# Two groups of small loads in a DMA-filled elementwise kernel on Trainium2

## The chip, the cores and the metric

The kernel runs on one core of a Trainium2 chip. The metric is the device time of one execution in microseconds (us). The kernel before took 1867.16 us in the median of 3 runs (1866.8 to 1867.26). The engines that matter here are VectorE (DVE), ScalarE (ACT), SyncE (SP), which does nothing but issue DMAs, and the sixteen DMA engines that carry out what SP issues.

## The reference

`pred` and `target` are 8192 x 8192 arrays of float32. The output is the Huber loss of each element:

```python
diff = pred - target
abs_diff = np.abs(diff)
return np.where(abs_diff <= 1.0, 0.5 * diff**2, abs_diff - 0.5)
```

Two arrays of 268 MB are read and one is written, with a few operations an element.

## The kernel before, in words

All three arrays are taken as flat and cut into 37 tiles of 128 rows. The list `widths` holds the columns of each: 9408 for tile 0, 12000 for tile 1, 14592 (`W`) for the next 34, and 6752 for the last. Tile `i` is one contiguous stretch of memory, so that a row is a contiguous run of 4 x width bytes.

One buffer, `mem`, takes 128 rows of 53184 columns of the on-chip memory. The functions `at_a(i)` and `at_b(i)` say where the pred and the target of tile `i` lie in it. Targets of even tiles start at column 0, those of odd tiles at 14592; preds of even tiles start at 29184, those of odd tiles end at 53184. The preds of two neighbouring tiles overlap in some columns (`covered`). The result of a tile is made in the place of its target, and is stored from there.

`load(i)` issues the DMAs of a tile on SP (line 80): pred, then target, each in one transfer of 7296 KB for a full tile, and in two parts for tiles 0, 34, 35 and 36. For the last tile both parts of pred go ahead of both parts of target. `store(i)` (line 85) writes the result, in one transfer, or two for the last tile.

`work(i, then)` computes a tile in pieces of some 5000 columns, of which each goes through five instructions: DVE subtracts (line 95), ACT takes the absolute value (96), DVE clamps it to 1 (100), ACT squares half of it (103), DVE combines the two with the maximum of (|d| - 0.5) and the square (107). `work` interleaves the pieces, and calls `then` behind the first subtractions, where the loads of the next tile are issued.

The order of the work is written out by hand (`manual_schedule`), and each engine runs its instructions in the order in which the program issues them. SP's order is therefore: the loads of tiles 0 and 1; then for each tile the store of the tile before, and the loads of the tile behind. An instruction of SP that waits holds up all that stand behind it. What each waits for is worked out by the framework from the columns that are read and written, and from the semaphores that it gives to the DMAs: eight of them, taken in turn. The loop is

```python
load(0)
load(1)
for i in range(n):
    if i > 0:
        store(i - 1)
    work(i, lambda: load(i + 1) if 0 < i < n - 1 else None)
store(n - 1)
```

Of the kernel before, what the change touches and what calls it, by code (L numbers as in the profile page):

```python
# [1 line left out]

# [4 lines left out]


@with_exitstack
def kernel(  # L10
    ctx: ExitStack,
    tc: tile.TileContext,
    pred: bass.AP,
    target: bass.AP,
    out: bass.AP,
):
    nc = tc.nc
    P = 128
    fp32 = mybir.dt.float32
    Alu = mybir.AluOpType  # L20
    Act = mybir.ActivationFunctionType
    SQRT_HALF = 0.70710678118654752

    total = pred.shape[0] * pred.shape[1] // P
    W = 14592
    GAP = 9408
    R = W - GAP
    widths = [GAP, W - R // 2] + [W] * 34
    widths.append(total - sum(widths))
    n = len(widths)  # L30
    starts = [sum(widths[:i]) * P for i in range(n)]

    def block(x, i):
        flat = x.rearrange("r m -> (r m)")
        return flat[starts[i] : starts[i] + P * widths[i]].rearrange("(p m) -> p m", p=P)

    pool = ctx.enter_context(tc.tile_pool(name="memory", bufs=1))
    mem = pool.tile([P, 3 * W + GAP], fp32, name="mem")

    def at_a(i):
        return 3 * W + GAP - widths[i] if i % 2 else 2 * W

    def at_b(i):
        return W if i % 2 else 0

    def covered(i):  # L50

        if i + 1 >= n:
            return (0, 0)
        lo = max(at_a(i), at_a(i + 1))
        hi = min(at_a(i) + widths[i], at_a(i + 1) + widths[i + 1])
        return (lo - at_a(i), hi - at_a(i)) if hi > lo else (0, 0)


    def parts(i):
        w = widths[i]  # L60
        if i == n - 3:
            return [(w - 2 * R, w), (0, w - 2 * R)]
        if i in (0, n - 2, n - 1):
            return halves(w)
        return [(0, w)]

    def halves(w):
        h = w // 32 * 16
        return [(0, h), (h, w)]

    def view(base, lo, hi):
        return mem[:, base + lo : base + hi]

    def load(i):
        order = [(x, part) for part in parts(i) for x in "pt"]
        if i == n - 1:
            order = [(x, part) for x in "pt" for part in parts(i)]
        for x, (lo, hi) in order:
            src, base = (pred, at_a(i)) if x == "p" else (target, at_b(i))
            nc.sync.dma_start(out=view(base, lo, hi), in_=block(src, i)[:, lo:hi])  # L80

    def store(i):
        w = widths[i]
        for lo, hi in halves(w) if i == n - 1 else [(0, w)]:
            nc.sync.dma_start(out=block(out, i)[:, lo:hi], in_=view(at_b(i), lo, hi))

    def split(lo, hi, size):
        k = -((lo - hi) // size)
        edges = [lo + (hi - lo) * j // k // 16 * 16 for j in range(k)] + [hi]
        return list(zip(edges[:-1], edges[1:]))  # L90


    def subtract(i, lo, hi, at):
        a, d = view(at_a(i), lo, hi), view(at_b(i), lo, hi)
        nc.vector.tensor_tensor(out=d, in0=a, in1=d, op=Alu.subtract)  # L95
        nc.scalar.activation(out=d, in_=d, func=Act.Abs)  # L96

    def square(i, lo, hi, at):
        d, t = view(at_b(i), lo, hi), view(at_a(i) + at, 0, hi - lo)
        nc.vector.tensor_scalar(  # L100
            out=t, in0=d, scalar1=-1.0, scalar2=1.0, op0=Alu.max, op1=Alu.min
        )
        nc.scalar.activation(out=t, in_=t, func=Act.Square, scale=SQRT_HALF)  # L103

    def combine(i, lo, hi, at):
        d, t = view(at_b(i), lo, hi), view(at_a(i) + at, 0, hi - lo)
        nc.vector.scalar_tensor_tensor(  # L107
            out=d, in0=d, scalar=-0.5, in1=t, op0=Alu.add, op1=Alu.max
        )

    def pieces(i, lo, hi):


        c0, c1 = covered(i)
        c0, c1 = max(lo, c0), min(hi, c1)
        if c1 <= c0:
            k = -((lo - hi) // (R // 2 if i < n - 1 else R // 4))
            return [], [(i, x, y, x) for x, y in split(lo, hi, -((lo - hi) // k))]
        x, y = (lo, c0) if c0 > lo else (c1, hi)
        m = max(c1 - c0, (y - x) // 32 * 16)  # L120
        rest = [(x, x + m), (x + m, y)] if y > x + m else [(x, y)]
        return [(i, c0, c1, x)], [(i, x, y, x) for x, y in rest]

    def work(i, then):

        todo, held = [], []
        for part in parts(i):
            first, rest = pieces(i, *part)
            todo += first + rest
            held += first  # L130
        mid, end = [], []
        if held:
            subtract(*todo.pop(0))
        then()
        while todo or mid or end or held:
            if todo:
                piece = todo.pop(0)
                subtract(*piece)
                mid.append(piece)
                if len(mid) < 2 and todo:  # L140
                    continue
            if mid:
                piece = mid.pop(0)
                square(*piece)
                end.append(piece)
                if len(end) < 2 and (todo or mid):
                    continue
            combine(*end.pop(0))
            mid += held
            held = []  # L150

    ctx.enter_context(tc.manual_schedule())

    load(0)
    load(1)
    for i in range(n):
        if i > 0:
            store(i - 1)
        work(i, lambda: load(i + 1) if 0 < i < n - 1 else None)
    store(n - 1)  # L160


# [1 line left out]
_INS = ['pred', 'target']  # L164
_OUTS = [((8192, 8192), 'float32')]


# [23 lines left out]
```

## Time and profile before

| | |
|---|---|
| median of 3 runs | 1867.16 us |
| the profiled execution | 1866.7 us |
| its span | 1864.9 us |
| DVE busy | 1408.3 us (76%) |
| ACT busy | 912.5 us (49%) |
| DMA moved | 805.37 MB, 432 GB/s over the span |
| DMA issues | 120, by their counts in the list of issues |

The page has the span in 40 slices, with a digit for the busy share of each engine in tenths and the rate of the DMA in GB/s. The chain of work that ended last goes back from the end to what released each step; in order of time, each row gives its start, its length and its engine. SPq is SP's queue: a row of it is the issue of a DMA, and the landing comes later. The list of issues gives the time from issue to landing. A view of several stretches gives, for each stretch, its length, the busy time of DVE, ACT and POOL, the clock of TensorE (not used here), the DMA's share and its rate.

### The profile page before, as it was taken

The page shows a single profiled execution, that of the slowest core. Times are in us where ns is not written, and L with a number is a line of the kernel's source. Part 1 is how long each engine was busy: PE and PEld are TensorE (multiplying, and loading weights), DVE is VectorE, ACT ScalarE, POOL GpSimd, SP SyncE. Part 2 cuts the span into 40 slices and gives each one's busy share as a digit, 9 for nine tenths or more (in the row PEclk, how much of TensorE's full clock was granted, in tenths as well). Part 3 has the DMA queues.
Part 4 walks back from the last instruction along what each step waited for, and adds up shares of the span by engine and source line. Part 5 has one row for each costly group of instructions (what it writes and reads, how often), then busy time and mean ns, then how long its engine had stood idle before and what let it go on. Part 6 is the DMA issues. An engine that isn't in the chain of part 4 may idle for free.

```text
span 1864.9 us, 960 instructions
## 1 busy us (share of the span) xinstructions
DVE 1408.3 (76%) x357; ACT 912.5 (49%) x239; POOL 0.2 (0%) x4
## 2 busy tenths in 40 slices
DVE  5677777777788777777778877777777887777986
ACT  3455444444555545444455554544445555454554
POOL 0000000000000000000000000000000000000000
DMA  9999999999999999999999999999999999999999
GB/s 421 418 436 431 436 431 432 437 427 436 438 428 434 439 428 435 438 429 433 438 428 436 438 428 435 438 428 436 438 427 437 436 429 437 435 429 436 428 437 393
DMA packets 17287, 805.37 MB, mean 432 GB/s; under 512 B 1920, under 2 KB 1920, under 8 KB 1920
## 3 DMA queue, kind: packets, MB, share of 16 engines
q1 hardware_dynamic: 17280, 805.31, 99.9%
q14 instruction: 7, 0.06, 0.0%
HBM read 536.87 MB, written 268.44 MB: 432 GB/s over the span
## 4 chain that ended last, share of the span: by engine, by line
DMA 56%; DVE 26%; ACT 13%; issue 4%; another core or an unknown queue 1%; SPq 0%; DVEq 0%
DMA mem<-in_target_dram 32%; DMA out_dram<-mem 24%; DVE mem L107 11%; DVE mem L95 11%; ACT mem L103 8%; ACT mem L96 4%; DVE mem L100 3%; SPq L80 0%; DVEq L95 0%
## 5 line engine op out<-in xcount | busy, mean ns | idle before, releaser
L96 ACT ACTIVATE mem<-mem 128x5184 f32<-128x5184 f32 (+8 forms) x119 | 459.2, 3874 | 756.3 <-DVE mem L95 756.2
L95 DVE TENSOR_TENSOR mem<-mem 128x5184 f32<-128x5184 f32 (+8 forms) x119 | 558.5, 4743 | 336.2 <-DMA mem<-in_target_dram 336.2
L107 DVE SCALAR_TENSOR_TENSOR mem<-mem 128x5184 f32<-128x5184 f32 (+8 forms) x119 | 564.4, 4745 | 74.5 <-ACT mem L103 70.6
L103 ACT ACTIVATE mem<-mem 128x5184 f32<-128x5184 f32 (+8 forms) x119 | 456.7, 3864 | 169.2 <-DVE mem L100 169.2
L100 DVE TENSOR_SCALAR mem<-mem 128x5184 f32<-128x5184 f32 (+8 forms) x119 | 292.0, 2453 | 34.9 <-ACT mem L96 29.9
L96 ACT ACT_TABLE_LOAD x1 | 1.3, 1283 | 14.6 <-DMA mem<-in_target_dram 14.6
L175 POOL MEMSET const-bfloat16-1.0<- 128x1 bf16 x1 | 0.1, 103 | 0.0
L175 POOL MEMSET const-uint8-127<- 128x1 uint8 x1 | 0.1, 102 | 0.0
L175 POOL MEMSET const-float32-0.0<- 128x1 f32 x1 | 0.1, 100 | 0.2 <-issue 0.2
L175 POOL MEMSET const-float32-1.0<- 128x1 f32 x1 | 0.1, 99 | 0.0
## 6 DMA issues: line engine op xcount, KB each, us to landing
out_dram<-mem SPq DMA_DIRECT2D x34, 7296.0 KB, 26.5
mem<-in_pred_dram SPq DMA_DIRECT2D x32, 7296.0 KB, 28.7
mem<-in_target_dram SPq DMA_DIRECT2D x32, 7296.0 KB, 34.4
mem<-in_pred_dram SPq DMA_DIRECT2D x2, 3648.0 KB, 27.6
mem<-in_target_dram SPq DMA_DIRECT2D x2, 3648.0 KB, 25.5
mem<-in_pred_dram SPq DMA_DIRECT2D x1, 6000.0 KB, 36.8
mem<-in_target_dram SPq DMA_DIRECT2D x1, 6000.0 KB, 51.5
out_dram<-mem SPq DMA_DIRECT2D x1, 6000.0 KB, 24.6
```

The source lines that it names most:

```text
L95: nc.vector.tensor_tensor(out=d, in0=a, in1=d, op=Alu.subtract)
L96: nc.scalar.activation(out=d, in_=d, func=Act.Abs)
L100: nc.vector.tensor_scalar(out=t, in0=d, scalar1=-1.0, scalar2=1.0, op0=Alu.max, op1=Alu.min)
L103: nc.scalar.activation(out=t, in_=t, func=Act.Square, scale=SQRT_HALF)
L107: nc.vector.scalar_tensor_tensor(out=d, in0=d, scalar=-0.5, in1=t, op0=Alu.add, op1=Alu.max)
L175: nc = _bacc.Bacc("TRN2", target_bir_lowering=False, num_devices=1)
```

## The change

A function `few_rows(at)` is added. It issues eight loads on SP, of 1, 2, 4, 6, 8, 10, 12 and 14 rows and of 16, 32 and so on to 128 columns, from the first rows of `pred` into `mem` from column `at` on, side by side. They are read by nothing. It is called twice: behind the loads of tile 1, ahead of the first store, into the columns behind tile 0's target (`GAP` is 9408); and behind the loads of the last tile, ahead of the store of tile 35, into the columns behind the last tile's pred.

```diff
+    def few_rows(at):
+        for k, rows in enumerate((1, 2, 4, 6, 8, 10, 12, 14)):
+            w = 16 * (k + 1)
+            nc.sync.dma_start(
+                out=mem[0:rows, at : at + w], in_=block(pred, 0)[0:rows, 0:w]
+            )
+            at += w
...
     load(0)
     load(1)
+    few_rows(GAP)
     for i in range(n):
         if i > 0:
             store(i - 1)
-        work(i, lambda: load(i + 1) if 0 < i < n - 1 else None)
+        if i == n - 2:
+            load_last = lambda: (load(i + 1), few_rows(2 * W + widths[n - 1]))
+            work(i, load_last)
+        else:
+            work(i, lambda: load(i + 1) if 0 < i < n - 1 else None)
     store(n - 1)
```

The instructions of DVE and ACT and their order are the same in both kernels; SP has 16 DMAs more.

## The prediction

> **What bounds the kernel now.** I read the page's slices first, then the DMA queues, the chain, the queue of SP (the engine that issues every DMA), and last the stretches in which the rate of the DMA sinks.
>
> ```profile
> DVE  5677777777788777777778877777777887777986
> ACT  3455444444555545444455554544445555454554
> ...
> DMA  9999999999999999999999999999999999999999
> GB/s 421 418 436 431 436 431 432 437 427 436 438 428 434 439 428 435 438 429 433 438 428 436 438 428 435 438 428 436 438 427 437 436 429 437 435 429 436 428 437 393
> ...
> q1 hardware_dynamic: 17280, 805.31, 99.9%
> ```
>
> VectorE and ScalarE have room in every slice; the DMA has none in any, and its queue is 99.9% busy. So the end moves by what is taken from or given to the DMA, and time in which its sixteen engines have nothing is lost for good. The steady rate comes from the chain: the store issued at 607.61 lands at 634.09, the one at 710.94 at 737.42, and two tiles (six transfers of 7296 KB) take 103.33 us between: 17.22 us each, 434 GB/s. The mean is 432.
>
> Next, the two places of the change. The first answer below is SP's queue around the first store, the second around the end, the third the chain at the start, the fourth the rates.
>
> ```profile
> 44.92 0.35 SPq L85 DMA_DIRECT2D out_dram<-mem  x1
> 58.21 0.33 SPq L80 DMA_DIRECT2D mem<-in_pred_dram  x1
> 66.40 0.33 SPq L80 DMA_DIRECT2D mem<-in_target_dram  x1
> ```
>
> ```profile
> 1822.72 0.81 SPq L80 DMA_DIRECT2D mem<-in_target_dram  x2
> 1831.85 22.48 SPq L85 DMA_DIRECT2D out_dram<-mem  x3
> ```
>
> ```profile
> 44.90 10.28 another core or an unknown queue
> 55.27 12.81 DVE mem L95 x3
> ```
>
> ```profile
> 40.00:48.00 8.00, 4.90 (x2) 2.06 (x1) 0.00 (x0) 1.00 1.03 444
> 48.00:51.00 3.00, 0.00 (x0) 0.00 (x0) 0.00 (x0) 1.00 0.81 352
> 51.00:54.00 3.00, 0.00 (x0) 0.00 (x0) 0.00 (x0) 1.00 0.99 269
> ```
>
> The reader is to see an order. The first store (tile 0) is issued at 44.92, while the second tile's target load is still moving: that load lands at 44.90 + 10.28 = 55.18. The store is therefore already queued when the load ends, and the engines run on without a pause. The same holds at the end: the store of tile 35 is issued at 1831.85, and by the DMA view the last piece of target (issued 1823.1, landing 15.7 later) lands at 1838.8. Both new groups are put on SP just ahead of these two stores.
>
> The fourth answer shows something else. Between 51 and 54 us the rate falls to 269 GB/s. The pred load of tile 1 took 14.2 us (landing 39.9 after the one before at 25.7), the target load of the same 6000 KB took 15.3 (39.9 to 55.18): a **stall of 1.1 us**, in its last packets, with the store waiting behind it.
>
> **The change, step by step.** Nothing is removed; 16 DMAs of 57 rows a group are added.
>
> *Bytes.* A group moves 57 rows of 64 to 512 bytes, about 20 KB: 0.05 us at 434 GB/s.
>
> *Packets.* The trace has no data packet that small. The nearest rows are the 4-byte semaphore packet (9 ns) and the 13504-byte row (505 ns). A DMA of 14 rows can use at most 14 engines and one of 1 row only one, so the engine with the most work has eight data packets a group, 0.1 to 4 us by those ends. 512 bytes are nearer to the first, and I take 0.5 us. Most of it lies in the gap worked out next, which covers about 1.5 us.
>
> *Free columns.* The first group writes columns 9408 to 9983 and the second 35936 to 36511, which no tile uses then. The target load of tile 2 and DVE's first subtraction of tile 2 get waits for the first group, which has landed some 10 us (the load) and over 40 us (the subtraction) earlier: nothing.
>
> *Waits.* This is the step that counts. The compiled order of both kernels shows that DMAs take eight semaphores in turn, and that an instruction which takes one again waits until the DMA eight before it has landed. In the kernel before, that one is nearly three tiles old. Sixteen DMAs in two groups of eight bring it close. First group: the loads of tiles 0 and 1 are DMAs 0 to 5, so the eight small ones are 6 to 13; the third to the sixth wait for tile 0's four loads, the seventh for tile 1's pred, **the eighth for tile 1's target**. Behind the eighth stand, in SP's order, the store of tile 0, then tile 2's pred and target. Second group: its fifth to eighth wait for the four loads of the last tile, and behind the eighth stands the store of tile 35. So each store can be issued only when the last load ahead of it has landed and the DMA has run dry.
>
> *Price of running dry.* The trace has one such start, that of the kernel. The first load is issued at 0.73 and lands 8.2 us later; the next of the same 2352 KB lands 5.6 us after it. So 8.2 - 5.6 = 2.6 us lie between an issue on an empty queue and full flow. Ahead of it comes the issue of the eighth small load: SP's rows are 0.33 to 0.97 us for 128 rows; 14 rows may cost less, and I take 0.4. With 0.05 between issues and 0.03 to wake, a gap costs 0.03 + 0.4 + 0.05 + 2.6 = **3.1 us**. By bounds: without the issue, and with the bare 1.0 us from that first issue to the first byte (the stretch to 1.70 us shows 0 GB/s) plus 0.3 from a last packet to its landing, 1.4; with 0.97 for the issue, 3.7. I take 3.1 because the start of the kernel is the only row of the same thing.
>
> [...]
>
> *First gap.* Tile 1's target would now be followed by loads, not by a store, so its 1.1 us stall should go: +3.1 - 1.1 = +2.0. The computation of tile 1 starts no later, and tile 2's loads still queue ahead of need, so nothing else waits.
>
> *Second gap.* At the end the store of tile 35 lands at 1831.85 + 24.2 = 1856.05, 17.25 us after the load before it: no stall to gain there. +3.1. The last two stores queue behind it (the last combine ends at 1854), so the end moves by the whole of it.
>
> **Sum:** +2.0 + 3.1 = +5.1 us. The profiled execution took 1866.7 us (span 1864.9), so 1871.8 of its own time; the runs' median lies 0.46 higher at 1867.16, so the predicted time is **1872.3 us**, +0.27%. A measurement of this kernel can tell about 0.2% (3.7 us) from no change, so the forecast lies just beyond that, at 1870.9.
>
> **Rivals.**
>
> *A: the small loads stagger the engines, and later stalls go.* After the first gap there are further stalls of the same kind. From 115.30 (a store lands) to 219.83, 323.65, 427.40 and 530.75 the intervals are 104.53, 103.82, 103.75 and 103.35 us against 103.33 in the steady state: 1.2 + 0.5 + 0.4 + 0.0 = 2.1 us, with 0.3 more between 66.40 and 115.30, 2.4 in all. The landings of one transfer's sixteen engines lie 0.9 us apart in the first loads and 3.4 at the end; as they spread, the stalls cease. Small loads that give some engines more packets than others could bring that spread at once. For it: the stalls die out exactly as the spread grows. Against it: seven of the eight are done before the store is even issued, so the gap swallows the stagger. Price: 5.1 - 2.4 = +2.7, 1869.9 us, not slower by what can be told. It decides where the eighth load and the restart leave over 2 us of spread. With the cheap gaps of the bound above (1.4 each, 3.4 less for both) it would be -0.7, 1866.5.
> [...]
>
> *B: the stall comes back.* The store starts on all engines at once out of the gap, in lockstep, and pays the 1.1 us there, as tile 1's target did, or the small packets cost nearer 505 ns and outlast their cover. For it: lockstep is when the stalls are seen. Against: the stall lay in load packets with a store behind, and there is no load now. Price: +1.1 for the first gap and up to 1.1 for the second, +7.3, 1874.5 us.
>
> *C: SP isn't held,* because the loads land before their turn comes. Then only packets are added, and the stagger could take away all stalls (1.1 + 2.4): -3.0, 1864.2 us. Against it: the last target load cannot land before 1838.8, and its waiter stands ahead of the store that today goes at 1831.85. Even all stalls together are 3.5 us, so a gain over 0.2% is nearly excluded.
>
> **Chances.** Forecast 0.50 (its own range 1870.6 to 1873.4), A or cheaper gaps 0.24, B 0.22, C 0.04. The range runs from inside A to B: 1868.4 to 1874.6. Its bounds in full, gaps of 1.4 to 3.7 with all or no stalls, are 1866 to 1876; what I leave out at both ends is under 0.2. Faster by over 0.2%: 0.02. Within: 0.24 and the lower edge of the forecast, less what of A lies higher, 0.28. Slower: 0.70.
>
> **What would show it.** SP's queue after the change should have the eighth small load right at the landing of tile 1's target (about 54.1, without the stall) and the first store some 0.45 us later, near 54.6 instead of 44.92; the rate in a stretch of 3 us from there should fall to a third or less. The same near 1841 with the store of tile 35, 9 us later than now. The first store should land near 68.4 instead of 66.40. Intervals of two tiles from 500 us on should stay at 103.33. The forecast is wrong if the stores are issued while loads still move, if the intervals before 500 us also become 103.33 (A), or if a gap is under 2 us.

## The result, and the profile after

The changed kernel takes 1872.74 us (median of 7 runs, 1872.51 to 1873.88), the kernel before 1866.97 in the same comparison (7 runs, 1866.44 to 1867.26). The ratio is 1.0032, with a 95% interval of 1.0021 to 1.0044: slower by 5.8 us. The profiled execution took 1872.51 us with a span of 1870.7, against 1866.7 and 1864.9.

From the page of the kernel after, the rate of the DMA by slices and its queue:

```profile
GB/s 419 411 412 438 431 431 434 437 426 436 438 432 428 439 436 428 434 438 433 430 436 437 433 428 438 437 428 433 438 432 433 433 438 430 433 437 432 430 433 374
...
q1 hardware_dynamic: 17508, 805.36, 99.7%
```

The DMA has 228 packets more, 0.05 MB more, and is busy 99.7% of the span where it was 99.9%. Two slices lost more than the 9 GB/s by which others differ either way: the third (412 for 436), which lies just behind the first group, and the last (374 for 393), which has the second. The slice with the first group lost only 7 (411 for 418), since a stall goes there too, as the prediction says.

SP's queue in the kernel after, around the first store and around the end:

```profile
54.13 0.32 SPq L86 DMA_DIRECT2D mem<-in_pred_dram  x1
54.56 0.38 SPq L94 DMA_DIRECT2D out_dram<-mem  x1
57.13 0.35 SPq L80 DMA_DIRECT2D mem<-in_pred_dram  x1
68.19 0.33 SPq L80 DMA_DIRECT2D mem<-in_target_dram  x1
```

```profile
1827.07 15.53 SPq L86 DMA_DIRECT2D mem<-in_pred_dram  x8
1843.02 14.78 SPq L94 DMA_DIRECT2D out_dram<-mem  x3
```

The row at 54.13 is the eighth small load. Tile 1's target landed at 54.11, so it goes at once, and the first store behind it is issued at 54.56 instead of 44.92. It lands at 68.11 instead of 66.38, and the next load goes at 68.19 instead of 66.40. At the end the eight loads take 15.5 us of SP's queue, and the store of tile 35 goes at 1843.02 instead of 1831.85.

What the DMA did meanwhile, in stretches cut to the two gaps (length, busy time of DVE, ACT and POOL, clock, DMA share, GB/s). The kernel after, then the kernel before at the first place:

```profile
53.80:55.40 1.60, 1.20 (x1) 0.00 (x0) 0.00 (x0) 1.00 0.02 5
...
1842.20:1843.80 1.60, 1.60 (x3) 1.60 (x2) 0.00 (x0) 1.00 0.04 10
```

```profile
53.80:55.40 1.60, 0.13 (x1) 0.00 (x0) 0.00 (x0) 1.00 0.93 400
```

For 1.6 us the DMA moves 5 and 10 GB/s, where it moved 400 at the first place before. These are the two gaps, in one line each; stalls that come back behind the first are a second cost.

How late the kernel after runs, from the landings of stores in the two traces:

| landing of | before | after | late by |
|---|---|---|---|
| the first store | 66.38 | 68.11 | 1.7 |
| the store of tile 1 | 115.29 | 118.14 | 2.8 |
| the store of tile 10 | 582.41 | 585.73 | 3.3 |
| the store of tile 34 | 1822.70 | 1826.20 | 3.5 |
| the store of tile 35 | 1856.05 | 1861.79 | 5.7 |
| the last store | 1864.11 | 1869.92 | 5.8 |

The steps are 1.7 at the first gap, 1.1 at the next two turns (0.9 in tile 2's target load, which has a store behind it, and 0.2 in that store), 0.7 spread over the tiles behind, and 2.2 at the second gap.

### The profile page after: what moved, and what is told of

Its sections match the earlier page's. It is cut to its first block, busy times and chain, and to the rows that moved or that the text cites. A ratio compares the mean times of both kernels' runs of the same rounds, so it can differ in the third digit from the quotient of the medians.

```text
span 1870.7 us, 983 instructions
## 1 busy us (share of the span) xinstructions
DVE 1408.2 (75%) x357; ACT 912.5 (49%) x239; POOL 0.2 (0%) x4
## 3 DMA queue, kind: packets, MB, share of 16 engines
q1 hardware_dynamic: 17508, 805.36, 99.7%
## 4 chain that ended last, share of the span: by engine, by line
DMA 58%; DVE 25%; ACT 12%; issue 4%; another core or an unknown queue 0%; SPq 0%; DVEq 0%
DMA mem<-in_target_dram 31%; DMA out_dram<-mem 25%; DVE mem L116 11%; DVE mem L104 11%; ACT mem L112 8%; ACT mem L105 4%; DVE mem L109 3%; DMA mem<-in_pred_dram 2%; SPq L80 0%; DVEq L104 0%
```

## The experiments

The theory under test, H: the time comes from SP being held, since a DMA that takes one of eight semaphores again waits for the one eight before it (in the kernel after, the third to the sixth small load go 0.02 us behind the landings of tile 0's four loads), and the DMA runs dry twice. The rival P: the small loads cost by their number. A second pair concerns what follows a gap. L: a gap starts all sixteen engines level, and level engines stall at the turns from loads to stores until they have drifted apart. G: a gap costs its own length and no more. The last four runs ask whether staggered engines avoid the stalls, and whether that pays.

| kernel | median us | before, same chip | ratio, 95% interval |
|---|---|---|---|
| groups of six | 1867.49 | 1867.13 | 1.0003, 0.9994 to 1.0011 |
| groups of seven | 1873.12 | 1867.13 | 1.0032, 1.0020 to 1.0045 |
| first group alone | 1870.78 | 1867.13 | 1.0019, 1.0011 to 1.0028 |
| second group alone | 1869.56 | 1867.13 | 1.0013, 1.0004 to 1.0022 |
| hold without the groups | 1873.30 | 1867.20 | 1.0033, 1.0020 to 1.0045 |
| one hold in the middle | 1873.89 | 1867.20 | 1.0038, 1.0025 to 1.0050 |
| staircase, 4576 columns | 1870.66 | 1867.20 | 1.0020, 1.0011 to 1.0029 |
| staircase, 2288 columns | 1868.78 | 1867.20 | 1.0007, 0.9998 to 1.0016 |
| spaced staircase, 4576 | 1868.72 | 1867.03 | 1.0007, 0.9998 to 1.0016 |
| spaced staircase, 3424 | 1868.59 | 1867.03 | 1.0008, 0.9999 to 1.0017 |

### Six loads or seven

```diff
-        for k, rows in enumerate((1, 2, 4, 6, 8, 10, 12, 14)):
+        for k, rows in enumerate((1, 2, 4, 6, 8, 10)):
```

> Each group is cut to its first six loads (1 to 10 rows), so that by the compiled order the first store waits for tile 1's pred (which lands at 39.9 us) and no longer for its target, and the store of tile 35 for the first part of the last target (landing near 1834.8), not the second (1838.8). Theory H (the time comes from the hold, which lets the DMA run dry twice): no gap, so within 0.7 us of the kernel before, about 1867 us. Rival P (the small loads cost by their number, 5.8 us for 16): 12 of them, +4.3, about 1871.3 us.

The second kernel keeps the 12 as well.

> Each group is cut to its first seven loads (1 to 12 rows). The store behind the group takes the eighth semaphore, and so itself waits for the last target load: the hold stays, with one issue less in each gap. H: two gaps, shorter by some 0.4 us each, +4.8 to +5.8, about 1872.2 us, and a step of 5 us against the kernel with six. P: 14 of 16 loads, +5.1, but only 0.7 more than with six.

Measured: +0.4 us with six (its interval includes no change) and +6.0 with seven. Twelve small loads cost next to nothing, and the seventh of both groups together brings some 5.6 us. SP's queue with six loads, and the rate of the same 1.6 us:

```profile
4.07 22.17 SPq L86 DMA_DIRECT2D mem<-in_pred_dram  x6
45.14 0.38 SPq L94 DMA_DIRECT2D out_dram<-mem  x1
```

```profile
53.80:55.40 1.60, 0.00 (x0) 0.00 (x0) 0.00 (x0) 1.00 0.91 382
```

The small loads still wait on SP (22 us of its queue), but the wait ends before the store is due: it goes at 45.14, and the DMA never runs dry. P is refuted. With seven, the hold sits in the store itself, which takes the semaphore of tile 1's target; the count decides, not which instruction waits.

### One group at a time

```diff
-            load_last = lambda: (load(i + 1), few_rows(2 * W + widths[n - 1]))
+            load_last = lambda: load(i + 1)
```

> The first group alone. In the trace of after, the landings run 1.7 us late behind the first gap (first store), 2.8 late at the store of tile 1, and 3.5 late from the middle on. H with the returning stalls: +3.5, about 1870.5 us, of which some 2 are the gap and the rest stalls at the turns from load to store that come back once the engines start level. P: half, +2.9, with nothing that grows behind the first tiles.

The other kernel drops the first call instead.

```diff
-    few_rows(GAP)
```

> The second group alone. In the trace of after, the store of tile 35 lands 2.25 us later than by the shift up to it. H: +2.3, about 1869.3 us, all between the last target load and the store of tile 35, nothing before. P: half of 5.8, +2.9.

Measured: +3.65 and +2.43 us, 6.1 together where both gave 5.8. The first group costs more, though both hold one store by one landing. In the trace of the first alone, the first store lands at 68.12, 1.7 late, and the store of tile 1 at 118.00, 2.7 late: the loss grows after the gap has been paid. With the second alone, all of it lies between the last target load and the store of tile 35 (2.5 us).

### The hold without the groups

```diff
+    def again(i):
+        at = at_b(i) + widths[i] - 128
+        nc.sync.dma_start(
+            out=mem[0:14, at : at + 128],
+            in_=block(target, i)[0:14, widths[i] - 128 : widths[i]],
+        )
...
     load(1)
+    again(1)
...
+            load_last = lambda: (load(i + 1), again(i + 1))
```

> No small loads into free columns; in each of the two places one load of 14 rows and 128 columns that loads the last columns of the tile's target a second time (the same values), and so waits until that target has landed; the store stands behind it. H: the hold alone gives the whole change, +5.5 to +6, about 1872.9 us, as with sixteen loads. P: 2 of 16 loads, +0.7, about 1867.8 us.

Measured: +6.1 us. Two small loads that write nothing new, but must wait for a target, do what sixteen did. Its SP queue shows the pair at 54.30 and 54.83, as after has it at 54.13 and 54.56:

```profile
54.30 0.40 SPq L84 DMA_DIRECT2D mem<-in_target_dram  x1
54.83 0.37 SPq L92 DMA_DIRECT2D out_dram<-mem  x1
```

### One hold in the middle

```diff
+        if i == 20:
+            load_held = lambda: (load(i + 1), again(i + 1))
+            work(i, load_held)
```

> The same single held load, but once and in the middle: behind the loads of tile 21, ahead of the store of tile 20. There the landings of one transfer lie 3.3 us apart and the turns from load to store cost nothing. Theory L (a gap starts all engines level, and level engines stall at the turns until they have drifted apart): 2.2 us for the gap, then some 0.8 at the first store's end, 1 at the next turn and more behind, in all +3.5 to +5.5, with a spread under 1 us behind the gap and stalls in the tiles that follow. Rival G (the stalls belong to the first tiles, and a gap costs its length alone): +2.3 and no stalls behind.

Measured: +6.7 us for a single hold, above L's range (5.5) and far above G's 2.3. The same stores in the chain, start of the issue and time to the landing. First the kernel with the hold, then the kernel before:

```profile
1021.55 26.49 DMA out_dram<-mem
1124.88 30.68 DMA out_dram<-mem
1232.70 26.89 DMA out_dram<-mem
1337.40 26.70 DMA out_dram<-mem
1441.87 26.47 DMA out_dram<-mem
```

```profile
1020.93 26.47 DMA out_dram<-mem
1124.26 26.47 DMA out_dram<-mem
1227.60 26.48 DMA out_dram<-mem
1330.93 26.48 DMA out_dram<-mem
1434.26 26.49 DMA out_dram<-mem
```

Add the two numbers of a row for the landing. Before, the landings are 103.33 us apart, row after row. With the hold at 1082, the intervals are 107.52, 104.03, 104.51 and 104.24: 4.2 us over in the first, then 0.7, 1.2 and 0.9. The landing records say the same of the engines: the sixteen of one transfer lie 4.1 us apart ahead of the hold, 0.6 behind it, and grow to 3.6 by the load of tile 27. The transfers that lose time are the held store (2.9), the target load after it (1.1), the store behind that (0.2), and later target loads that stand ahead of a store (0.4, 0.3, 1.0, 0.2, 0.9). No pred load, which has a load behind it, loses any. G is refuted.

The held store's 2.9 us divide by the packet records. Its last packets on all engines, ahead of a load, take 2.6 to 3.3 us where 2.15 is their time: some 0.8 is a stall at the turn from store to load (0.7 in the mean of the sixteen, nearly 1.0 on the engine that ended last). So the dry DMA itself costs some 2.1.

### Engines staggered without a hold

```diff
     load(0)
+    stairs(4576)
     load(1)
...
+    def stairs(w):
+        lo = 0
+        for rows in (2, 4, 8, 12):
+            nc.sync.dma_start(
+                out=mem[lo : lo + rows, GAP : GAP + w],
+                in_=block(pred, 0)[lo : lo + rows, 0:w],
+            )
+            lo += rows
```

> The kernel before with four more loads between tile 0's and tile 1's, of 2, 4, 8 and 12 rows of 4576 columns, which give some engines up to four rows (2.7 us) more than others; nothing is held by them. L: the engines are 2.7 us apart from there on, the stalls at the turns go (1.1 at tile 1's target, 2.4 behind), the last engine does 2.7 us more: -0.8, about 1866.3 us. G: the stalls stay, +2.7, about 1869.8 us.

The second has `stairs(2288)`.

> The same with 2288 columns: 1.35 us apart. L: part of the stalls go, between -1.2 and +0.8, about 1867 us; G: +1.35, about 1868.5 us.

Measured: +3.5 and +1.6 us, even more than G's figures; but the traces say that it is not for G's reason. With 4576 columns tile 1's target load lost nothing (1.1 before), nor did any transfer up to 256 us: the engines were 2.9 us apart, and the stalls were gone as L says. What was off is the price. The added packets of 18304 bytes took 0.8 to 1.8 us each, where 681 ns is what their size needs (as the pair below shows), so that the staircase cost 5.0 us and not 2.7. With 2288 columns the spread was 1.2 us; the stall of tile 1's target was gone, but 0.2 to 0.5 came back at the turns of the tiles behind.

In both, added rows lie side by side on chip. The next pair puts them four apart, and has loads of 2, 4, 6 and 8 rows:

```diff
-        lo = 0
-        for rows in (2, 4, 8, 12):
+        for at, rows in enumerate((2, 4, 6, 8)):
             nc.sync.dma_start(
-                out=mem[lo : lo + rows, GAP : GAP + w],
-                in_=block(pred, 0)[lo : lo + rows, 0:w],
+                out=mem[at : at + 4 * rows : 4, GAP : GAP + w],
+                in_=block(pred, 0)[0:rows, 0:w],
             )
-            lo += rows
```

The first has `stairs(4576)`, the second `stairs(3424)`.

> The staircase again, 4576 columns, but with rows four apart in the on-chip memory (2, 4, 6 and 8 rows), since in the staircase of neighbouring rows the added packets took 0.8 to 1.8 us where their size at 27 GB/s asks for 0.68, and the whole cost 5.0 us in place of 2.7. If neighbouring rows share a way into the memory, rows four apart do not: the packets take about 0.7 us, the spread is 2.7 us, the 3.5 us of stalls go as before, and the kernel comes to -0.8 to +0.5, about 1867.0 us. If the packets are slow for another reason (few engines, short rows), +3.4 as with neighbouring rows, about 1870.6 us.

> The same with 3424 columns, a spread of 2.0 us. With rows that do not share: 2.0 us added, most of the 3.5 us of stalls gone, -1.0 to +0.5, about 1866.8 us; otherwise between the two staircases of before, about 1869.6 us.

Measured: +1.7 and +1.6 us. Every added packet now took exactly 681 ns (512 with 3424 columns), where with neighbouring rows a packet took 0.8 to 1.8 us. That neighbouring rows share a way into the memory was the author's guess; the runs show the packets' times and not what lengthens them.

The chain of the kernel with 4576 spaced columns:

```profile
45.13 23.31 DMA out_dram<-mem
68.46 24.28 DMA mem<-in_target_dram
92.76 24.36 DMA out_dram<-mem
117.13 34.42 DMA mem<-in_target_dram
194.00 26.43 DMA out_dram<-mem
220.45 34.42 DMA mem<-in_target_dram
```

The first store lands at 68.44, the store of tile 1 at 117.12, that of tile 3 at 220.43: 48.68 and 103.31 us, where the kernel before had 48.9 and 104.5. The stalls behind the first store are gone, and at 430 us this kernel is only 0.4 us late. But the first stall remained (1.1 at tile 1's target, with eight engines staggered and eight still level). And the staggered engines lost more later: 8-KB packets of the instruction queue run in both kernels, and beside each one data packet takes 0.2 to 0.7 us more (in the kernel before 2.39 to 2.82 us, where 2.15 is the time of a row of 58 KB). Two of those behind 430 us (at 931 and 1603) fell in the transfers in which the last landing slipped, by 0.6 and 0.8 us; in the kernel before, the last landing did not move at such packets. No version here beats the kernel before: what a stagger costs the last engine (2.7 us, and the two slips) is about what the stalls cost (3.5).

## Why the prediction was right, point by point

The forecast was 1872.3 us, +5.1; the measurement is 1872.74, +5.8. The direction, the mechanism and the place of the two gaps were right. The price of a gap was put too high, and the stalls that come back behind the first were put at nothing; the two errors have opposite signs.

*The DMA as the bound, and the store's issue.* Right. SP's queue has the eighth load at 54.13 and the store at 54.56 (forecast 54.1 and 54.6), the store of tile 35 at 1843.02 (forecast near 1841, where 2.0 us were to be lost by then and 3.5 were), and the DMA at 5 and 10 GB/s in the gaps. One sign that the prediction named did not show: a rate of a third or less over 3 us from the gap. The view gives 404 GB/s:

```profile
54.00:57.00 3.00, 2.80 (x2) 0.00 (x0) 0.00 (x0) 1.00 0.95 404
```

The view counts a packet where it starts: the store's first packets start at 55.43 and its second ones at 56.82, so that two rounds of sixteen are counted in these 3 us. A stretch cut to the gap shows it; one of 3 us does not.

*Small packets, bytes, columns.* Right in that they cost nothing: six loads a group are +0.4 us within the interval. They are cheaper than assumed: a packet of 64 to 512 bytes took 11 to 26 ns (one of the 114 took 176), so eight of them, each with a semaphore packet of 9, 0.2 us in place of 0.5.

*The stall at tile 1's target.* Right: the load took 14.16 us instead of 15.29.

*Price of running dry, 3.1 us.* The term that was mis-sized. Measured: 2.3 for the second gap (19.53 us from landing to landing where 17.22 is the store's time), some 2.1 for the first, and the same in the middle. The first store took 14.00 us from landing to landing where 11.1 is its time. Some 0.8 of the 2.9 was the stall at its end, where the last packets took 1.84 to 2.50 us instead of 1.39: 0.7 more in the mean, nearly 1.0 on the engine that ended last. So the 2.1 is good to some 0.2 us, and whether that gap was under 2 us, which the prediction named as a sign against itself, can't be told. The issue of the eighth load (0.32) was near the 0.4 taken. The start of the kernel was not the same thing after all: its first packets took 0.8 to 1.8 us where 0.70 is their time, while the first packets of the held store took 1.40 where 1.39 is theirs. The nearest row contained a slow start that the restart in the middle of a run did not have.

*"So nothing else waits" behind the first gap.* This failed. The stall that left tile 1's target came back: 0.8 at the first store's end and 1.1 at tile 2's target (0.25 there before), and the tiles up to 530 us lost 2.6 in place of 2.1. Intervals from the chain of after, from the store of tile 1 on:

```profile
89.57 28.57 DMA out_dram<-mem
118.15 34.73 DMA mem<-in_target_dram
195.32 27.08 DMA out_dram<-mem
222.42 34.49 DMA mem<-in_target_dram
299.33 26.95 DMA out_dram<-mem
326.30 35.11 DMA mem<-in_target_dram
```

The landings 118.14, 222.40 and 326.28 are 104.26 and 103.88 us apart against 103.33. This is rival B's mechanism, with its price too low and its place too narrow: the held store paid 0.8 at its end and the turns behind it paid more, some 2.5 us in all behind the first gap where B had 1.1. At the second gap no stall came: only stores follow there, and the last two took 4.07 and 4.05 us from landing to landing (4.02 and 4.04 before). From 534 us on the two-tile intervals stayed within 0.2 us of 103.33, as the prediction said.

*The sum.* Forecast 3.1 - 1.1 + 3.1 = 5.1. Measured 2.1 - 1.1 + 2.3 = 3.3 for the gaps and the first stall, and 2.5 for stalls that came back: 5.8. So the total was near partly by luck: 1.8 us too much for the gaps and 2.5 too little for the stalls.

*Rival A* was refuted for this change: the spread behind the first gap was 0.6 us, and stalls went on. Its idea, that spread engines do not stall, fits the first staircase (2.9 us apart, nothing lost up to 256 us), but the gap does the opposite of a stagger: 0.85 us ahead of it, 0.6 behind, and at the second gap 3.3 and 0.3. The prediction's argument against it, that seven of the eight loads are done before the store is issued, holds for their packets (the last of the seven's ran at 53.73) and not for their landings, which came 0.2 us apart from 54.08 to 55.19, three of them ahead of the store's issue at 54.56. *Rival C* was refuted: SP was held.

Left open: why level engines stall at a turn at all. The packet records show that the last packets before a turn stretch on all engines at once (2.5 to 3.2 us at tile 1's target in the kernel before, where 1.77 is their time); they do not show what holds them. Nor is it clear why the first stall went with twelve staggered engines and stayed with eight.

## What to carry to other kernels

Here, with the DMA's queue busy for 99.9% of the span, what counted of an added transfer was not its bytes but whether its issue held up the next large one: six small loads in a group cost nothing that can be told from noise (+0.4 us), and the seventh brought 5.6 us for the two groups because semaphores dealt in turn made the store wait for the newest load. Before adding DMAs ahead of a queue, count back by the number of semaphores and look at what that DMA is. A gap can cost more than its length: here 2.1 to 2.3 us, and up to 4.6 more (the hold in the middle) where turns between loads and stores follow and level engines have to find their spread again. At the end of the kernel, with only stores behind, it cost its length alone (2.3 us).

## What the runs showed of the hardware

- With the landings of one transfer 0.6 to 2.9 us apart, single turns between loads and stores lost up to 1.1 us (before: 1.1 at tile 1's target, 0.8 at tile 3's; after: 1.1 at tile 2's). With 3 us or more between them, the turns of these two kernels lost under 0.1, but for one of 0.17 (after, the target load issued at 999.1) and the second gap. In the first staircase, 2.9 us apart, nothing was lost up to 256 us; in the spaced one, with 2.7 us but eight of the engines still level, tile 1's target lost 1.1. The steady 17.22 us a transfer (434 GB/s) came after some ten tiles (from 530 us on in both kernels), and was lost for some tiles by the one hold in the middle, with the landings 4.1 us apart ahead of it and 0.6 behind.
- A packet of 64 to 512 bytes took 11 to 26 ns, but for one of 114 (176 ns).
- Loads of a few neighbouring rows took 0.8 to 1.8 us a packet of 18304 bytes, rows four apart 0.68.
- Beside an 8-KB packet of the instruction queue one 58-KB packet took 2.39 to 2.82 us where 2.15 is its time, at all seven in the run of the kernel before. In the spaced staircase the last landing slipped by 0.6 and 0.8 us at two of them, in the kernel before at none.
